# The last six input tiles of the last FFN down-projection as Strassen blocks

## Chip, cores and metric

One Trainium2 chip, one core. The metric is device time of one launch in microseconds (us), the median of several runs.

## What is computed

A two-layer diffusion backbone over 1024 latent tokens and 256 context tokens, model width 1024, everything in float32. Layer 0 mixes tokens with a bidirectional gated linear recurrence, layer 1 with a gated short convolution; each is followed by a gated convolutional FFN (width 2816), and the stream ends in a root-mean-square norm. The part that matters here is the end:

```python
def conv_ffn(h, w_up, conv_w, conv_b, w_down, conv_fn):
    g, v = jnp.split(h @ w_up, 2, axis=-1)
    return (jax.nn.silu(conv_fn(g, conv_w, conv_b)) * v) @ w_down
...
x = x + (gf * conv_ffn(hl, f_w_up[l], f_conv_w[l], f_conv_b[l], f_w_down[l], latent_hconv))
...
return rms_norm(x, final_g)
```

## The kernel before

Activations lie as channels by tokens: `x` is 128 partitions by 8 channel tiles by 1024 tokens, and `H[0]`, `H[1]` are the two halves of 512 tokens. Every matrix product keeps float32 accuracy by splitting both operands into a high and a low part (`split`: ScalarE writes the high part, VectorE the difference), so that `mm` issues three matmuls of 128 x 128 weights with up to 512 tokens each: high-high, high-low, low-high.

Large products go as one level of Strassen's scheme in Winograd's form: `block_items` makes seven weight blocks out of two weight tiles (raw DMA, up to two VectorE additions, then the split), `STEPS` runs the seven products in the order 1, 5, 6, 3, 7, 2, 4, and products 1, 6, 7, 4 add up in one PSUM bank whose running sum is read after each of them. The activation side has seven combinations of four tiles each, named "11", "21", "22", "T1" to "T4"; a table `ROLES` says which product takes which.

The down-projection of the FFN has 22 input tiles. In `v_post`, a pair of gated tiles of the up-projection is turned into its seven combinations by four VectorE subtractions and stored to the DRAM scratch `bd` (`store_blocks`); this is done for the first 16 tiles. The last six are stored plainly to the scratch `ad`. `down` then runs two groups of eight tiles as Strassen blocks (`down_blocks`, four pairs of output tiles each), loading the combinations back through `act_item` (which splits them into operand slots), and finishes with the six left-over tiles by plain products: eight output tiles, each six weight tiles against 512 tokens. In the last layer this rest runs in three pieces, tokens 0 to 511, 512 to 767 and 768 to 1023; the weights of an output tile (768 columns) are loaded and split anew for each piece. After each product, `residual` adds the gated result to `x` on VectorE (a SCALAR_TENSOR_TENSOR from PSUM, called the residual below) and `norm_sq` squares it on ScalarE and adds it on VectorE into `acct`. `final` of a finished piece (sums by matmuls with ones, square root, reciprocal, a broadcast by matmul, four multiplies, four stores) is called while the next piece runs.

No engine runs in program order: the class `Plan` records every operation with an assumed cost, works out for each when it is due (TensorE's order is fixed, and dues run back from it), and emits each engine's instructions in the order that a greedy list schedule gives. The emitted order is then fixed for VectorE, ScalarE, TensorE and the DMA queue of SyncE alike, and each of them works strictly in that order. Line 165 is the place where `Plan` emits, so every profile row carries it; the rows are told apart by tile names: `banks` is PSUM, `wh`/`wl` the split weights, `bh`/`bl` the split activations, `raw` and `s` staging tiles, `xd` the saved stream.

Of the kernel before, what the change touches and what calls it, by code (L numbers as in the profile page):

```python
# [183 lines left out]
def hybrid_kernel(ctx: ExitStack, tc: tile.TileContext, out, xs, cs, c, cc, ada, vecs,  # L184
# [115 lines left out]
    def wsrc(key):  # L300
        kind = key[0]
        if kind in ("x", "xc"):
            return wx[key[1]]
        if kind == "g":
            return wg[key[1]]
        if kind == "o":
            return wo[key[1]]
        if kind == "ri":
            return wri[key[1]]
        if kind == "bo":  # L310
            return wbo[key[1]]
        return wdn[key[1], key[2], :, 2 * D:]

    def dot(dst, raw, bt, eng=None):
# [10 lines left out]
    def weight_item(key):  # L325
        src = wsrc(key)
        n = src.shape[-1]

        def prep(sl, raws):
            hi, lo = flat(sl[0][0], sl[0][2], len(sl))[:, :n], flat(sl[0][1], sl[0][2], len(sl))[:, :n]  # L330
            split(hi, lo, raws[0].tile[:, :n], weight_hi[0])
            return hi, lo
        return Item(key, [Raw(src)], -(-n // HALF), prep)

    def block_items(name, src1, src2, again):

# [114 lines left out]

    accs = {}

    def norm_sq(s, m):
        n = s.stop - s.start
        if m == 0:
            accs[s.start] = acct[:, s.start // HALF, s.start % HALF:s.start % HALF + n]
            act(accs[s.start], x[:, m, s], AF.Square)
        else:
            q = tmp(n)  # L460
            act(q, x[:, m, s], AF.Square)
            if s.start >= 768 and m == KD - 1:
                accs["end"] = q
            else:
                add(accs[s.start], q, accs[s.start], V)
# [621 lines left out]
    def residual(l, sl, m, s, ps, keep):  # L1087
        stt(x[:, m, s], ps, gcol(l, sl, m), x[:, m, s])
        if keep:
            nc.sync.dma_start(xd[:, m, s], x[:, m, s])  # L1090
        norm_sq(s, m)

    def load_res(m):
        nc.sync.dma_start(x[:, m], xd[:, m])
# [60 lines left out]
    def ffn(l, second, i):  # L1155
        cw = [[vcol("f_conv_w", (l * 3 + t) * KFF + j) for t in range(3)] for j in range(KFF)]
        us = []

        def g_post(j0):
            def post(row, h, a, b):  # L1160
                j = j0 + row
                if a is not None:
                    add(a, a, b)
                    b = a
                o = x[:, j % 8, H[h]]
                act(o, b, AF.Identity, bias=vcol("f_conv_b", l * KFF + j), scale=cw[j][1])
# [24 lines left out]

        def store_blocks(q, a, b):

            def put(i, t):
                nc.sync.dma_start(bd[:, i:i + 2, q], t.rearrange("p (h n) -> p h n", h=2))
            b11, b12, b21, b22 = a[:, H[0]], a[:, H[1]], b[:, H[0]], b[:, H[1]]
            nc.sync.dma_start(bd[:, 0, q], b11)
            put(1, b)
            sub(b11, b12, b11)
            sub(b12, b22, b12)  # L1200
            sub(b22, b22, b11)
            sub(b21, b21, b22)
            put(3, a)
            put(5, b)
        for j in range(0, KFF, 2):
            us.append(blocks(("up", l, j), wup[l, j], wup[l, j + 1], g_post(j), 1 if j == 0 else 2 if j == 2 else 0))
            us.append(blocks(("up", l, KFF + j), wup[l, KFF + j], wup[l, KFF + j + 1],
                             v_post(j), 1 if j == 0 else 2 if j == 2 else 0))
        ends = run_blocks(us, second, 8 if l else 24, 2)
        call(gate_bias, l, 5)  # L1210
        return down(l, ends, i)

    def act_item(key, src, load_after, slots, after, pool="raw"):

        def prep(sl, rs):
            for j in (0, 1):
                split(*bslot(slots[j]), rs[0].tile[:, j * HALF:(j + 1) * HALF])
        items[key] = Item(key, [Raw(src, load_after, pool)], 0, prep, after)

    def down(l, ends, i):  # L1220
# [5 lines left out]
        for g in range(2):  # L1226
# [8 lines left out]
            for q in range(4):  # L1235
                steps = down_blocks(l, g, q, role)
                ends = [unit(f, *(acts[p] if q == 0 else []), k) for p, f, k in steps]
        R = released()
# [5 lines left out]
        last, second = i is None, None  # L1244
        if not last:
            begin, first, second = block_norm(i, R[12:] + R[:12])
        pieces = [H[0], slice(HALF, 768), slice(768, SEQ)] if last else H
        for z, s in enumerate(pieces):
            h, o = s.start // HALF, s.start % HALF
            for m in range(KD):  # L1250
                def f(w, m=m, h=h, o=o, s=s):
                    n = s.stop - s.start
                    ps = bank()[:, :n]
                    for k in range(6):
                        rh, rl = bslot(R[6 * h + k])
                        mm(ps, w, slice(k * P, (k + 1) * P), rh[:, o:o + n], rl[:, o:o + n], k == 0, k == 5)
                    residual(l, 5, m, s, ps, not last)
                acts = [("act", l, "t", h, kk) for kk in range(3)] if m == 0 and o == 0 else []
                unit(f, *acts, ("dt", l, m, z))
                if z and last and m == 1:  # L1260
                    fin = final(pieces[z - 1])
                    call(fin[0])
                elif z and last and m == 3:
                    call(fin[1])
                elif z and not last:
                    if m == 0:
                        call(begin)
                    if m == 1:
                        call(norm_cols, i, 1, 0, 1, "norm_mix_g")
                        call(first)  # L1270
        if last:
            for f in final(pieces[-1]):
                call(f)
        return second

    def down_blocks(l, g, q, role):

# [167 lines left out]
```

## Time and profile before

| | us |
|---|---|
| median of 3 runs (lowest to highest) | 2079.51 (2079.14 to 2079.75) |
| profiled execution | 2082.59 |
| its span, first to last instruction | 2080.8 |
| TensorE busy with matmuls in the span | 2036.8 (98%) |
| VectorE busy | 1764.5 (85%) |
| ScalarE busy | 1049.3 (50%) |

The profiled execution is 3.08 us (0.15%) above the median. In the timeline a row has its start, the time it was busy, engine, operation, tiles and shape, how many were merged, and in brackets the idle time before it with what ended it. Instructions of one engine overlap a little, so what one costs its engine is the distance from start to start.

### The profile page before, as it was taken

Reading aid. Unit: us, or ns where it says so; the run is one execution under the profiler, and the core shown is the slowest. Engines: PE = TensorE matmul, PEld = TensorE weight load, DVE = VectorE, ACT = ScalarE, POOL = GpSimd, SP = SyncE. Lnnn points to the kernel's source line nnn. Section 1 sums busy time; section 2 is a strip of 40 time slices with the busy share of each in tenths; the row PEclk is TensorE's granted clock in tenths of the full one; section 3 lists DMA queues with packets and bytes.
Section 4 is the critical chain, followed back from the end, with each engine's and each line's share of the span. In section 5 each row is a group of like instructions: output and inputs, shape, how many; then the busy total and the mean of one; then the engine's idle time right before and its main releaser. Section 6 shows DMA issues by size and latency. Waiting matters only on the chain.

```text
span 2080.8 us, 25029 instructions
## 1 busy us (share of the span) xinstructions
PE 2036.8 (98%) x9218; PEld 1681.5 (81%) x9218; DVE 1764.5 (85%) x2624; ACT 1049.3 (50%) x1574; POOL 0.2 (0%) x4
## 2 busy tenths in 40 slices
PE   8899989999999999999999999999999999999998
PEld 6688877787888888878888788888888888878888
DVE  7998999979888888798769988858988887688867
ACT  6366878546544444535255433435644444464345
POOL 0000000000000000000000000000000000000000
PEclk9999999999999999999999999999999999999999
DMA  7544222551334455565361345652243443474345
GB/s 298 185 169 162 71 81 84 193 167 48 126 132 157 156 174 173 174 199 162 95 194 66 114 164 197 231 192 75 83 136 128 142 137 108 137 236 142 111 140 164
DMA packets 103418, 307.05 MB, mean 148 GB/s; under 512 B 10368, under 2 KB 14720, under 8 KB 103168
## 3 DMA queue, kind: packets, MB, share of 16 engines
q1 hardware_dynamic: 103296, 305.46, 44.6%
q8 instruction: 72, 1.18, 0.2%
q14 instruction: 50, 0.41, 0.1%
HBM read 248.80 MB, written 56.62 MB: 147 GB/s over the span
## 4 chain that ended last, share of the span: by engine, by line
PE 84%; DVE 9%; ACT 4%; DMA 2%; issue 1%; SPq 0%; DVEq 0%; ACTq 0%
PE banks L165 84%; ACT mx L165 2%; DVE x L165 2%; DVE mx L165 2%; DVE u L165 2%; DVE bl L165 2%; DMA x<-in_xs 1%; DVE wl L165 1%; DMA s<-bd 1%; ACT L165 1%; ACT bh L165 1%; DMA raw<-in_wg 0%; DVE uc L165 0%; DVE ul L165 0%; DVE acct L165 0%
## 5 line engine op out<-in xcount | busy, mean ns | idle before, releaser
L165 PE MATMUL banks<-bl,wh 128*128 128x512 f32 (+1 forms) x2720 | 1052.2, 387 | 11.0 <-DVE bl L165 10.9
L165 PE MATMUL banks<-bh,wh 128*128 128x512 f32 (+1 forms) x2720 | 1054.3, 388 | 3.2 <-ACT wh L165 1.6
L165 PE MATMUL banks<-bh,wl 128*128 128x512 f32 (+1 forms) x2720 | 1051.0, 386 | 2.6 <-DVE wl L165 2.5
L165 PEld LDWEIGHTS banks<-bl,wh 128*128 128x128 f32 x2720 | 511.6, 188 | 124.7 <-DVE bl L165 21.6
L165 PEld LDWEIGHTS banks<-bh,wh 128*128 128x128 f32 x2720 | 511.8, 188 | 109.0 <-ACT wh L165 2.0
L165 PEld LDWEIGHTS banks<-bh,wl 128*128 128x128 f32 x2720 | 511.6, 188 | 108.1 <-DVE wl L165 7.3
L165 ACT ACTIVATE wh<-raw 128x512 fp32r<-128x512 f32 (+2 forms) x386 | 275.6, 717 | 475.0 <-PE banks L165 394.7
L165 DVE TENSOR_TENSOR wl<-raw,wh 128x512 fp32r<-128x512 f32 (+2 forms) x386 | 303.2, 794 | 60.4 <-ACT wh L165 56.9
L165 DVE SCALAR_TENSOR_TENSOR x<-banks,mod,x 128x512 f32<-128x512 f32 (+1 forms) x184 | 132.6, 726 | 93.3 <-PE banks L165 92.3
L165 ACT ACTIVATE s<-banks 128x512 f32<-128x512 f32 x174 | 103.8, 596 | 195.0 <-PE banks L165 191.8
L165 ACT ACTIVATE wh<-s 128x512 fp32r<-128x512 f32 x216 | 135.5, 628 | 110.4 <-DVE s L165 63.7
L165 DVE TENSOR_TENSOR wl<-s,wh 128x512 fp32r<-128x512 f32 x216 | 148.5, 688 | 38.6 <-ACT wh L165 34.9
L165 DVE TENSOR_TENSOR s<-s,banks 128x512 f32<-128x512 f32 x158 | 107.8, 683 | 37.4 <-PE banks L165 36.9
L165 DVE SCALAR_TENSOR_TENSOR x<-s,vec,x 128x504 f32<-128x504 f32 x132 | 96.4, 740 | 10.2 <-ACT x L165 9.0
L165 DVE SCALAR_TENSOR_TENSOR acct<-acct,cb 128x1024 f32<-128x1024 f32 x69 | 84.1, 1218 | 4.5 <-DMA acct<-in_ada 4.5
L165 PE MATMUL banks<-uh,wh 128*128 128x512 f32 (+1 forms) x192 | 70.8, 369 | 8.1 <-ACT mx L165 7.0
L165 PE MATMUL banks<-ul,wh 128*128 128x512 f32 (+1 forms) x192 | 70.5, 367 | 3.1 <-DVE ul L165 3.1
L165 PE MATMUL banks<-uh,wl 128*128 128x512 f32 (+1 forms) x192 | 70.2, 366 | 0.0
L165 ACT ACTIVATE bh<-s 128x512 fp32r<-128x512 f32 x88 | 51.5, 624 | 35.3 <-DMA s<-bd 34.0
L165 ACT ACTIVATE bh<-x,cols 128x512 fp32r<-128x512 f32 x64 | 45.1, 721 | 42.1 <-DVE cols L165 27.3
L165 DVE TENSOR_TENSOR x<-x,s 128x512 f32<-128x512 f32 x90 | 61.0, 686 | 0.8
L165 DVE TENSOR_TENSOR bl<-s,bh 128x512 fp32r<-128x512 f32 x88 | 57.2, 684 | 5.0 <-ACT bh L165 5.0
(154 smaller groups left out, 1702.0 us busy)
## 6 DMA issues: line engine op xcount, KB each, us to landing
raw<-in_wup SPq DMA_DIRECT2D x92, 512.0 KB, 3.6
acct<-in_ada SPq DMA_DIRECT2D x69, 512.0 KB, 3.5
bd<-x SPq DMA_DIRECT2D x48, 512.0 KB, 3.2
s<-bd SPq DMA_DIRECT2D x44, 512.0 KB, 4.5
raw<-in_wdn SPq DMA_DIRECT2D x32, 512.0 KB, 4.4
raw<-in_wdn SPq DMA_DIRECT2D x40, 384.0 KB, 3.4
raw<-in_wbi SPq DMA_DIRECT2D x26, 512.0 KB, 4.1
u<-in_ada SPq DMA_DIRECT2D x24, 512.0 KB, 4.6
```

The costliest lines, as they stand in the source:

```text
L165: getattr(getattr(self.tc.nc, e), op)(*a, **k)
```

## The change

Three things belong together. In the last layer `v_post` calls `store_blocks` for the pairs 16, 18, 20 too (`bd` has eleven columns instead of eight). `down` ends for that layer in `last_group`, which runs the six tiles as a Strassen group of three tiles per block: products 1, 2, 6, 7, 4 of the four pairs of output tiles over 512 columns each in an order written out by hand, then products 5 and 3 for tokens 512 to 767 and once more for 768 to 1023. `late_items` prepares 28 weight blocks of 384 columns, with the raw weights of a pair loaded twice, once for products 1, 6, 2, 7, 4 and once for 5 and 3; the eight blocks of 5 and 3 stay in the eight weight slots through both halves. The rows of the weight array are permuted on input. The other layer's code is only moved (`down_rest`).

```diff
-    bd = dp.tile([P, 7, KD, HALF], F32, tag="bd", name="bd")
+    bd = dp.tile([P, 7, KFF // 2, HALF], F32, tag="bd", name="bd")
...
+    def late_items(name, src1, src2):
+        w = src1.shape[-1] // 2
+        raws = [[Raw(src1), Raw(src2)] for _ in range(2)]
...
+                if p in (5, 6):
+                    src = s[0] = stmp("w", w)
+                    add(src, a21, a22)
+                    if p == 6:
+                        sub(src, src, a11)
+                elif p == 7:
+                    src = a21
+                    sub(src, a11, a21)
+                elif p == 3:
+                    src = s[0]
+                    sub(src, src, a11)
+                    sub(src, a12, src)
+                else:
+                    src = {1: a11, 2: a12, 4: a22}[p]
+                split(hi, lo, src)
...
-                if j0 < 16:
+                if j0 < 16 or l:
                     if done[0] + done[1] == 4:
                         store_blocks(j0 // 2, x[:, j0 % 8], x[:, j0 % 8 + 1])
...
+    def last_group(l, ends, stored, last_up):
...
+                ps = st[q, 5 if p in (3, 5) else 1][:, H[p == 2]][:, :n]
+                for k in range(3):
+                    rh, rl = bslot(role3[p][k])
+                    mm(ps, w, slice(k * P, (k + 1) * P), rh[:, o:o + n], rl[:, o:o + n],
+                       p in (1, 2, 5) and k == 0, p in (2, 3, 4) and k == 2, skip_group_check=True)
+                r, h = to[p]
+                t = s if p in (5, 3) else H[h]
+                stt(x[:, 2 * q + r, t], ps, gcol(l, 5, 2 * q + r), x[:, 2 * q + r, t])
+                if p in (2, 4, 5, 3):
+                    end(2 * q + r, t)
...
+        for pq in "10 20 60 11 70 21 40 61 12 71 13 41 62 63 72 73 22 23 42 43".split():
+            put(int(pq[0]), int(pq[1]), H[0])
+        pieces = [slice(HALF, 768), slice(768, SEQ)]
+        for z, s in enumerate(pieces):
+            for n, (p, q) in enumerate(((5, 0), (5, 1), (3, 0), (3, 1), (5, 2), (5, 3), (3, 2), (3, 3))):
+                put(p, q, s)
+                if n == 2:
+                    fin = final(pieces[z - 1] if z else H[0])
                     call(fin[0])
...
+        for f in final(pieces[-1]):
+            call(f)
...
+    last = order[:16] + [16, 18, 20, 17, 19, 21]
```

The instruction order shows two places. The first is VectorE near the end, where the half-width residuals (256 tokens) begin. Before:

```order
L165 SCALAR_TENSOR_TENSOR x<-banks,mod,x 128x256
L165 TENSOR_TENSOR wl<-raw_2695,wh 128x768
L165 RECIPROCAL rt<-rt 128x4
L165 TENSOR_TENSOR s<-eye,rt 128x512
L165 SCALAR_TENSOR_TENSOR x<-banks,mod,x 128x256
L165 TENSOR_TENSOR wl<-raw,wh 128x768
L165 SCALAR_TENSOR_TENSOR x<-banks,mod,x 128x256
L165 TENSOR_TENSOR acct<-s,acct 128x256
L165 TENSOR_TENSOR x<-x,banks 128x2x512 x2
```

And with the change, at the same point:

```order
L165 TENSOR_TENSOR s<-raw 128x384
L165 SCALAR_TENSOR_TENSOR x<-banks,mod,x 128x256
L165 TENSOR_TENSOR wl_2694<-s,wh_2693 128x384
L165 TENSOR_TENSOR wl<-s,wh 128x384
L165 TENSOR_TENSOR s<-s,raw 128x384
L165 TENSOR_TENSOR s<-raw,s 128x384
L165 RECIPROCAL rt<-rt 128x4
L165 TENSOR_TENSOR s<-eye,rt 128x512
L165 TENSOR_TENSOR s<-raw 128x384
L165 SCALAR_TENSOR_TENSOR x<-banks,mod,x 128x256 x2
L165 TENSOR_TENSOR x<-x,banks 128x2x512 x2
L165 TENSOR_TENSOR wl<-s,wh 128x384
```

More and smaller instructions on the weights (`s` and `wl`, 384 columns) now stand between two residuals. The second place is SyncE's DMA queue where the up-projection of the last layer ends and the down-projection begins (`in_wdn` is the down weight). Before:

```order
L165 DMA raw<-bd 128x1024
L165 DMA s<-bd 128x1024
L165 DMA raw_2695<-bd 128x1024
L165 DMA raw<-in_wdn 128x1024
L165 DMA raw<-bd 128x1024
L165 DMA raw_2695<-bd 128x1024
L165 DMA s<-bd 128x1024 x3
L165 DMA raw<-in_wdn 128x1024
L165 DMA ad<-x 128x1024
L165 DMA s<-bd 128x1024
```

And with the change:

```order
L165 DMA raw_2695<-bd 128x1024
L165 DMA raw<-in_wdn 128x1024
L165 DMA raw<-bd 128x1024
L165 DMA raw_2695<-bd 128x1024
L165 DMA bd<-x 128x512
L165 DMA bd<-x 128x2x512
L165 DMA s<-bd 128x1024 x2
L165 DMA bd<-x 128x2x512
L165 DMA s<-bd 128x1024 x3
L165 DMA raw<-in_wdn 128x1024
```

Stores of the last pair's combinations (`bd<-x`) now stand ahead of the loads `s<-bd`, which bring the second half of the first group's activation blocks; one such load stood still earlier before.

## Rows read from the trace of the kernel before

**Rows 1.** The page, part 1: engines, busy time, share of the span.
```profile
PE 2036.8 (98%) x9218; PEld 1681.5 (81%) x9218; DVE 1764.5 (85%) x2624; ACT 1049.3 (50%) x1574; POOL 0.2 (0%) x4
```
**Rows 2.** Chain of waits, last 51 us: start, us, what.
```profile
2029.99 41.20 PE banks L165 x322
```
**Rows 3.** Windows: PE, PEld, DVE, ACT, POOL busy (count), PEclk, DMA share, GB/s.
```profile
1800.00:1850.00 50.00, 50.00 (x222) 41.40 (x222) 35.06 (x54) 26.28 (x45) 0.00 (x0) 1.00 0.53 164
1850.00:1900.00 50.00, 49.71 (x216) 39.52 (x215) 47.01 (x73) 19.82 (x33) 0.00 (x0) 1.00 0.61 205
...
2037.00:2071.20 34.20, 34.20 (x282) 33.66 (x280) 29.21 (x51) 22.36 (x43) 0.00 (x0) 1.00 0.57 181
```
**Rows 4.** Timeline: residuals at full and half width, first half-width matmul.
```profile
2005.55 0.75 DVE L165 SCALAR_TENSOR_TENSOR x<-banks,mod,x 128x512 f32<-128x512 f32 x1 [2.46 <-PE banks L165]
...
2009.63 0.75 DVE L165 SCALAR_TENSOR_TENSOR x<-banks,mod,x 128x512 f32<-128x512 f32 x1 [2.46 <-PE banks L165]
...
2033.90 0.28 PE L165 MATMUL banks<-bh,wh 128*128 128x256 f32 x1
...
2069.05 0.48 DVE L165 SCALAR_TENSOR_TENSOR x<-banks,mod,x 128x256 f32<-128x256 f32 x1 [0.37 <-PE banks L165]
...
2071.21 0.48 DVE L165 SCALAR_TENSOR_TENSOR x<-banks,mod,x 128x256 f32<-128x256 f32 x1 [0.76 <-PE banks L165]
```
**Rows 5.** Timeline of VectorE: neighbours that follow each other without idle time.
```profile
1109.60 2.49 DVE L165 TENSOR_TENSOR wl<-raw,wh 128x512 fp32r<-128x512 f32 x4
1112.01 0.68 DVE L165 TENSOR_TENSOR s<-s,banks 128x512 f32<-128x512 f32 x1
...
1962.32 0.74 DVE L165 SCALAR_TENSOR_TENSOR x<-banks,mod,x 128x512 f32<-128x512 f32 x1
1962.98 0.68 DVE L165 TENSOR_TENSOR raw<-raw,raw 128x512 f32<-128x512 f32 x1
...
2044.47 2.35 DVE L165 TENSOR_TENSOR x<-x,banks 128x1024 f32<-128x1024 f32 x2
2046.73 1.82 DVE L165 TENSOR_TENSOR wl<-raw,wh 128x768 fp32r<-128x768 f32 x2
...
2051.26 0.41 DVE L165 TENSOR_TENSOR acct<-s,acct 128x256 f32<-128x256 f32 x1
2051.59 0.47 DVE L165 SCALAR_TENSOR_TENSOR x<-banks,mod,x 128x256 f32<-128x256 f32 x1
2051.99 0.41 DVE L165 TENSOR_TENSOR acct<-s,acct 128x256 f32<-128x256 f32 x1
```
**Rows 6.** Timeline of VectorE: waits of its own in the last stretch.
```profile
2040.75 0.18 DVE L165 RECIPROCAL rt<-rt 128x4 f32<-128x4 f32 x1 [0.62 <-ACT rt L165]
...
2068.26 0.43 DVE L165 TENSOR_TENSOR acct<-s,acct 128x256 f32<-128x256 f32 x1 [0.15 <-ACT s L165]
```
**Rows 7.** Windows of 2 us around idle times of TensorE in layer 0.
```profile
106.00:108.00 2.00, 1.46 (x7) 0.88 (x5) 1.96 (x3) 1.22 (x2) 0.00 (x0) 1.00 0.97 406
108.00:110.00 2.00, 0.09 (x1) 0.12 (x1) 2.00 (x4) 1.47 (x4) 0.00 (x0) 0.87 0.68 236
...
114.00:116.00 2.00, 2.00 (x6) 1.54 (x5) 1.90 (x5) 1.96 (x4) 0.00 (x0) 0.50 0.15 14
116.00:118.00 2.00, 2.00 (x9) 1.64 (x8) 2.00 (x5) 2.00 (x3) 0.00 (x0) 0.92 0.77 264
366.00:368.00 2.00, 0.87 (x4) 0.65 (x4) 2.00 (x4) 2.00 (x5) 0.00 (x0) 1.00 0.38 110
```
**Rows 8.** Timeline of the DMA queue at the last layer's change from up to down.
```profile
1843.62 3.67 SPq L165 DMA_DIRECT2D s<-bd  x3
...
1849.16 0.42 SPq L165 DMA_DIRECT2D ad<-x  x1
```
**Rows 9.** Waits between 1840 and 1900 us: total, times, longest.
```profile
ACT bh L165 <- DMA s<-bd: 3.6, 3, 2.0
...
PE banks L165 <- DVE bl L165: 0.3, 1, 0.3
```

More of the change, by code (lines that the diff above doesn't have):

```diff
@@ L311, in wsrc @@
             return wbo[key[1]]
+        assert kind == "dt"
         return wdn[key[1], key[2], :, 2 * D:]
@@ L452, in hybrid_kernel, with norm_sq @@
     accs = {}
-    def norm_sq(s, m):
+    def norm_sq(s, m, first, end=False):
         n = s.stop - s.start
-        if m == 0:
+        if first:
             accs[s.start] = acct[:, s.start // HALF, s.start % HALF:s.start % HALF + n]
@@ L461, in norm_sq @@
             act(q, x[:, m, s], AF.Square)
-            if s.start >= 768 and m == KD - 1:
+            if end:
                 accs["end"] = q
@@ L1215, in prep @@
         def prep(sl, rs):
-            for j in (0, 1):
-                split(*bslot(slots[j]), rs[0].tile[:, j * HALF:(j + 1) * HALF])
+            for j, i in enumerate(slots):
+                split(*bslot(i), rs[0].tile[:, j * HALF:(j + 1) * HALF])
         items[key] = Item(key, [Raw(src, load_after, pool)], 0, prep, after)
@@ L1237, in down, with down_rest @@
                 ends = [unit(f, *(acts[p] if q == 0 else []), k) for p, f, k in steps]
+        if i is not None:
+            return down_rest(l, ends, i)
+        last_group(l, ends, stored, last_up)
+    def down_rest(l, ends, i):
         R = released()
@@ L1243, in down @@
                          ends[(sl + 1) // 4])
[L1244 to L1248, printed above, removed]
+        begin, first, second = block_norm(i, R[12:] + R[:12])
+        for z, s in enumerate(H):
             h, o = s.start // HALF, s.start % HALF
@@ L1256, in f @@
                         mm(ps, w, slice(k * P, (k + 1) * P), rh[:, o:o + n], rl[:, o:o + n], k == 0, k == 5)
-                    residual(l, 5, m, s, ps, not last)
+                    residual(l, 5, m, s, ps, True)
                 acts = [("act", l, "t", h, kk) for kk in range(3)] if m == 0 and o == 0 else []
                 unit(f, *acts, ("dt", l, m, z))
-                if z and last and m == 1:
-                    fin = final(pieces[z - 1])
+                if z and m == 0:
+                    call(begin)
@@ new lines, in down_rest, with end, step, f @@
+                if z and m == 1:
+                    call(norm_cols, i, 1, 0, 1, "norm_mix_g")
+                    call(first)
+        return second
+    def last_group(l, ends, stored, last_up):
+        role = roles[0]
+        rel = [(j, ends[t]) for t, (_, n) in enumerate(ROLES) for j in role[n]]
+        role3, acts, need = {}, {}, dict(ROLES)
+        for t, p in enumerate((1, 2, 6, 7, 4, 5, 3)):
+            at = rel[3 * t:3 * t + 3]
+            role3[p] = [j for j, _ in at]
+            acts[p] = [("act", l, 2, p, e) for e in range(2)]
+            for e, sl in enumerate((at[:2], at[2:])):
+                src = bd[:, stored[need[p]], 8:10] if e == 0 else bd[:, stored[need[p]], 10]
+                act_item(acts[p][e], src, last_up if t < 2 else ends[0] - 8, [j for j, _ in sl], sl[-1][1],
+                         "s" if t < 2 else "raw")
+        seen = []
+        def end(m, s):
+            seen.append(s.start)
+            n = seen.count(s.start)
+            norm_sq(s, m, n == 1, s.stop == SEQ and n == KD)
+        for q in range(4):
+            late_items(("db", l, 2, q), *[wdn[l, 2 * q + r, :, 2 * D:] for r in range(2)])
+        st = {}
+        to = {1: (0, 0), 5: (1, 1), 6: (0, 1), 3: (0, 1), 7: (1, 1), 2: (0, 0), 4: (1, 0)}
+        def step(p, q, s):
+            def f(w):
+                n, o = s.stop - s.start, s.start % HALF
+                if p in (1, 5):
+                    st[q, p] = bank()
+                ps = st[q, 5 if p in (3, 5) else 1][:, H[p == 2]][:, :n]
[8 more added lines that the diff above has]
+                    end(2 * q + r, t)
+            return f
+        def put(p, q, s):
+            unit(step(p, q, s), *acts.pop(p, []), ("db", l, 2, q, p))
+        for pq in "10 20 60 11 70 21 40 61 12 71 13 41 62 63 72 73 22 23 42 43".split():
[6 more added lines that the diff above has]
+                    fin = final(pieces[z - 1] if z else H[0])
@@ L1262, in down @@
                     call(fin[0])
-                elif z and last and m == 3:
+                elif n == 4:
                     call(fin[1])
[L1265 to L1274, printed above, removed]
+        for f in final(pieces[-1]):
+            call(f)
```

16 lines of the change are left out of this document (14 added, 2 removed).

## The prediction, made before the changed kernel was run

> **What bounds the kernel.** I read the page first: TensorE's matmuls fill 98% of the span, VectorE 85% [rows 1]. Over the whole kernel TensorE is the bound, and time saved on it should show. The chain of waits agrees: TensorE alone holds the last stretch for 41.20 us without a break, up to 2071.19 [rows 2]. The reader should then look at the stretches that the change touches, because a share over 2 ms hides them. In the windows [rows 3] VectorE is at 47.01 of 50 us where up- turns into down-projection, and at 29.21 of 34.20 over the half-width pieces at the end. TensorE is full in both, but VectorE has only 3 us to spare in the first and 5 us in the second. The change takes work from TensorE and gives work to VectorE in just these two places, so the question is which of them ends last there.
>
> **TensorE's share.** An output tile of 18 full-width matmuls takes 4.08 us, the distance of two residuals that TensorE ends [rows 4]; nine take 2.04. At half width 18 take 2.16 us [rows 4], nine 1.08. Before: 8 x 4.08 + 16 x 2.16 = 67.2 us. After: 20 x 2.04 + 16 x 1.08 = 58.1 us. **Saved: 9.1 us.**
>
> **VectorE's share.** Costs are distances from start to start [rows 5]: 0.60 us for 512 columns (2.41 for four), 0.66 for a residual of 512, 1.13 for 1024, 0.33 and 0.40 for an addition and a residual of 256. An instruction of 384 columns is not in the trace; it lies between 0.33 and 0.60, and I take the middle, 0.47. Added by the change: twelve subtractions in `store_blocks` (7.2 us, in the up-projection), nine more splits of activations (21 slots for 12; 5.4 us), twelve more residuals of 512 (7.9 us). The weights cost about the same in sum (28 splits and 24 additions of 384), but in more pieces, and those of products 5 and 3 come late: their eight slots must be free first.
>
> What matters is when it is due. In the new order of VectorE I counted from the residual of product 7 of the last pair, after which four full and sixteen half units remain on TensorE, up to the last residual. There stand 72 instructions: 6 residuals of 512 (4.0), 15 of 256 (6.0), 11 of 512 columns (6.6), 13 of 256 (4.3), 19 of 384 (8.9), 4 of 1024 (4.5), 2 of 2 x 256, priced as 512 (1.2), and 2 reciprocals (0.4, at 0.2 each by their 0.18 [rows 6]). The sum is 35.9 us. TensorE needs 4 x 2.04 + 16 x 1.08 = 25.4 us, and 2.7 us for the norms' matmuls: today from the first half-width matmul at 2033.90 to 2071.19 it takes 37.3 us [rows 2, 4], of which 16 x 2.16 = 34.6 are products. That makes 28.1 us. So the bound changes: VectorE's queue is 7.8 us longer than TensorE's. Before this point it keeps up: some 25 us of its rows against 15 units of 2.04 us.
>
> VectorE's waits come on top. In the last stretch it waited 0.62 us for ScalarE's square root and 0.15 us for a square [rows 6]; there are two square roots, and the weights of 5 and 3 pass from VectorE to ScalarE and back. Bounds: nothing (all filled by other rows) and 5 us (the idle time of this stretch before, 34.20 - 29.21 [rows 3]). I take 2.5 us, in the middle. **Lost at the end: 10.3 us.** What is late there is `wl` behind the multiplies of `final`, then residuals, for which TensorE waits before it may reuse a bank.
>
> Here a rule speaks for the change and against my sum. The Trainium skill, Perfetto Trace Analysis, "Identifying the Most-Contended Engine", says to relieve the engine of highest occupancy first; by it the 9.1 us would be a gain in full, since TensorE is at 34.20 of 34.20 and VectorE at 29.21. No run so far shows which is right after the change.
>
> **The change from up to down.** The queue of SyncE is strict. In the new order two stores `bd<-x` of the last pair stand before the loads `s<-bd`, and a third between them. The first three loads went out from 1843.62; the first plain store of that pair could go out only at 1849.16 [rows 8], since its data were made then. So the loads, and those behind them, may go out 5.5 us later. They were not early: ScalarE already waited 3.6 us for them, and TensorE lost 0.3 us to the split that follows [rows 9]. VectorE, which also has the last four subtractions (2.4 us) to do, has 3 us of room [rows 3] and cannot make it up. The other eight subtractions fall before 1850, where it was busy 35.06 of 50 us [rows 3], and cost nothing. Bounds: nothing (the queue catches up) and 7 us (5.5 in full, and 1.5 for the subtractions). **Lost: 3.5 us**, the middle.
>
> **TensorE's clock.** After an idle time of some 2.4 us around 108 us the granted clock fell to 0.50 and stayed there until about 116 [rows 7]: half the 2.4 GHz. After 1.1 us (366 to 368) it stayed at 1.00 [rows 7]. At the end one wait could be that long: after the broadcast of the first norm VectorE has two residuals, two multiplies of 1024 and a split to do (0.8 + 2.26 + 0.47 = 3.5 us) before TensorE gets its next weights. Some 6 us at half clock cost 3 us if nothing else waits, and nothing if VectorE is the bound anyway. I take **0.7 us**, nearer to nothing. The Trainium skill, TensorE: Matmul & The Clock Gate, "What's actually happening", also has just two levels and puts the fall down to lack of recent activity; the trace agrees.
>
> After the last residual nothing is changed. In both layers' up-projections the planner moves some stores and subtractions by a few places, because dues shift with the shorter end. I price this at nothing, with 1 us either way: the moved rows feed stores that are read much later, and the spare time of VectorE covers them, as between 1800 and 1850 [rows 3]. If that cover failed, each microsecond late would be one in the total.
>
> **Sum.** -9.1 + 10.3 + 3.5 + 0.7 = +5.4 us. The profiled execution (2082.59 us) is 3.08 us above the median, 2079.51; on the profile's scale this gives 2088.0, on the scale of the runs **2085.0 us**. A measurement of this kernel tells about 0.2% (4.2 us) from no change.
>
> **Rivals.**
> (a) TensorE stays the bound, VectorE's work slips into gaps: 2079.5 - 9.1 = 2070.4, faster. The place is the last 30 us; it decides if VectorE's 72 instructions take under 28.1 us, which would need the price of each to be a fifth lower. For it: VectorE had slack before. This is where the page's rule above would end. Against: 35.9 us by its own rows. Chance 0.06.
> (b) The two stalls eat the gain and no more: with no waits in the last stretch (7.8), none at the turn to down and no slow clock, -9.1 + 7.8 = -1.3, up to +4 when one of the two comes in part: 2078 to 2083.6, no change. For it: the bounds above. Chance 0.24.
> (c) The clock falls in both places and the waits reach their upper ends: -9.1 + 12.8 + 7 + 3 = +13.7, 2093, slower. Against: while TensorE is slow VectorE catches up. Chance 0.05.
> (d) The change doesn't do what it says, for instance if half-width matmuls were held by loading 128 x 128 weights each time. They were of half width before as well, at 0.12 us each, and their number halves; no chance of its own.
> My forecast, VectorE as the bound at the end and a lost microsecond or few at the turn, keeps 0.65: 2083.7 to 2090. Slower by over 0.2%: 0.65 + 0.05 = 0.70; within: 0.24; faster: 0.06. The range from 2079.0 to 2090.5 leaves out (a), (c) and a little of (b).
>
> **What would show it.** Right: at the end VectorE is busy nearly without a break over some 40 us, and TensorE's waits there name `wl`, `x` and `acct` on VectorE, some 10 us in sum; TensorE's busy time falls by about 9 us less what the clock takes; around 1865 TensorE waits a few us for `wh`, `bl` or `x`, behind `s<-bd`. Wrong: TensorE without idle time after 2030, or an end bounded by DMA (late `raw<-in_wdn`), or idle times before 1800 that were not there.

## The result, and the profile after

| | before | changed |
|---|---|---|
| median of the runs | 2079.63 us | 2090.85 us (2086.93 to 2093.60) |
| ratio | 1 | 1.0051, 95% interval 1.0038 to 1.0064 |
| profiled execution, its span | 2082.59, 2080.8 us | 2093.60, 2091.8 us |
| mean granted clock | 0.993 | 0.989 |

By the ratio the change makes the kernel 10.6 us slower (the two medians as they stand differ by 11.2 us), about twice the +5.4 us of the forecast, and the median lies 0.4 us above the upper end of the range. The direction and both places were right; each place cost more.

The page, part 1, of the changed kernel, against [rows 1]:
```profile
PE 2035.9 (97%) x9110; PEld 1675.1 (80%) x9110; DVE 1789.8 (86%) x2685; ACT 1050.7 (50%) x1587; POOL 0.2 (0%) x4
```
TensorE has 108 matmuls less, and yet its busy time falls by 0.9 us where 9 were forecast, less what the clock takes: matmuls that run at half clock count for longer. VectorE has 61 instructions and 25 us more.

To place the loss, three instructions serve as marks that all kernels here have in common: the last reciprocal of 128x4 ahead of the second layer's up-projection, the last residual of 512 before the down-projection's last group (it shows 1.37 us of idle time ahead of it), and the last residual of all. From the timeline of VectorE before (the third mark is in [rows 4]):
```profile
1430.41 0.18 DVE L165 RECIPROCAL rt<-rt 128x4 f32<-128x4 f32 x1 [0.34 <-ACT rt L165]
...
1976.99 0.75 DVE L165 SCALAR_TENSOR_TENSOR x<-banks,mod,x 128x512 f32<-128x512 f32 x1 [1.37 <-PE banks L165]
```
and after, with two residuals of the new units between:
```profile
1427.19 0.18 DVE L165 RECIPROCAL rt<-rt 128x4 f32<-128x4 f32 x1 [0.33 <-ACT rt L165]
...
1978.58 0.75 DVE L165 SCALAR_TENSOR_TENSOR x<-banks,mod,x 128x512 f32<-128x512 f32 x1 [1.37 <-PE banks L165]
...
2007.14 0.75 DVE L165 SCALAR_TENSOR_TENSOR x<-banks,mod,x 128x512 f32<-128x512 f32 x1 [0.63 <-PE banks L165]
2009.17 0.75 DVE L165 SCALAR_TENSOR_TENSOR x<-banks,mod,x 128x512 f32<-128x512 f32 x1 [0.69 <-PE banks L165]
...
2081.49 0.48 DVE L165 SCALAR_TENSOR_TENSOR x<-banks,mod,x 128x256 f32<-128x256 f32 x1
```
A unit of nine takes 2.03 us; 2.04 was priced. Up to the first mark the two profiles differ by 3.2 us in the other direction. From the first to the second mark ("the turn") the time went from 546.58 to 551.39 us, +4.8; from the second to the third ("the end") from 94.22 to 102.91, +8.7; behind the last residual from 9.6 to 10.3.

**The turn.** A window after, against [rows 3] (columns as there), and two short ones:
```profile
1850.00:1900.00 50.00, 47.62 (x195) 36.53 (x194) 43.75 (x69) 21.09 (x36) 0.00 (x0) 0.97 0.66 227
...
1858.00:1860.00 2.00, 2.00 (x6) 1.56 (x7) 1.39 (x3) 1.07 (x2) 0.00 (x0) 0.58 1.02 383
1860.00:1862.00 2.00, 2.00 (x6) 1.41 (x6) 2.00 (x4) 1.01 (x3) 0.00 (x0) 0.57 0.80 256
```
TensorE idles 2.1 us more than before in the first of these, and right behind the longest of its waits (first row below) the granted clock is at 0.58 and 0.57 for four microseconds, which is 1.7 us of clock. Some 1 us of the 4.8 I haven't placed. TensorE's waits, 1840 to 1900, then from 2020 on:
```profile
PE banks L165 <- ACT wh L165: 1.7, 1, 1.7
...
PE banks L165 <- DVE wl L165: 4.3, 2, 2.5
PE banks L165 <- DVE x L165: 2.4, 2, 1.8
PE banks L165 <- DVE acct L165: 2.1, 3, 1.0
PE banks L165 <- DVE s L165: 1.0, 1, 1.0
PE banks L165 <- DVE bl L165: 0.5, 1, 0.5
```
**The end.** These five sum to 10.3 us, all on VectorE, 8.8 of them for the buffers that the prediction named (`wl`, `x`, `acct`). The wait of 1.0 us for `s` stands in the kernel before as well. The chain of waits, which held one piece of TensorE of 41.20 us before [rows 2], changes hands:
```profile
2033.59 5.87 DMA raw<-in_wdn
...
2048.55 0.46 DVE wl L165
...
2050.09 0.60 DVE bl L165
...
2051.16 0.61 DVE acct L165
...
2051.81 7.63 PE banks L165 x28
...
2062.35 6.02 PE banks L165 x34
```
A load of raw weights holds the chain up to 2039, which the prediction had listed as a sign against it (more on it below). From there to 2051 the chain is VectorE almost without a break. Then come 28 matmuls in 7.63 us, and these ran at half clock, as windows of the same stretch show (PEclk is the third number from the end):
```profile
2044.00:2050.00 6.00, 3.52 (x24) 2.96 (x22) 6.00 (x12) 4.86 (x9) 0.00 (x0) 0.95 0.23 66
2050.00:2060.00 10.00, 9.04 (x33) 7.22 (x32) 7.33 (x16) 5.59 (x11) 0.00 (x0) 0.52 0.24 80
2060.00:2066.00 6.00, 3.65 (x18) 3.41 (x19) 5.90 (x12) 1.77 (x4) 0.00 (x0) 0.76 0.47 175
2066.00:2080.00 14.00, 11.48 (x79) 10.88 (x78) 10.35 (x22) 7.23 (x17) 0.00 (x0) 0.87 0.31 112
```
While TensorE crawls, VectorE, the supposed bound, stands and waits for it:
```profile
2057.77 0.48 DVE L165 SCALAR_TENSOR_TENSOR x<-banks,mod,x 128x256 f32<-128x256 f32 x1 [1.34 <-PE banks L165]
2059.47 2.35 DVE L165 TENSOR_TENSOR x<-x,banks 128x1024 f32<-128x1024 f32 x2 [1.22 <-PE banks L165]
```
So the two engines lose time in turn: VectorE makes TensorE wait, the clock falls behind the waits, and the slow matmuls make VectorE wait. Over the 42.0 us from 2039.49 to the last residual VectorE was busy for 35.3, so the sign "nearly without a break" held up to 2056 and not behind it.

### The profile page after: what moved, and what is told of

The parts are those of the page before. It is cut to its first block, busy times and chain, and to the rows that moved or that the text cites. A ratio compares the mean times of both kernels' runs of the same rounds, so it can differ in the third digit from the quotient of the medians.

```text
span 2091.8 us, 24892 instructions
## 1 busy us (share of the span) xinstructions
PE 2035.9 (97%) x9110; PEld 1675.1 (80%) x9110; DVE 1789.8 (86%) x2685; ACT 1050.7 (50%) x1587; POOL 0.2 (0%) x4
## 4 chain that ended last, share of the span: by engine, by line
PE 82%; DVE 10%; ACT 3%; DMA 2%; issue 1%; SPq 0%; DVEq 0%; ACTq 0%
PE banks L165 82%; DVE x L165 2%; DVE bl L165 2%; DVE mx L165 2%; ACT mx L165 2%; DVE u L165 2%; DMA s<-bd 1%; DVE wl L165 1%; DVE acct L165 1%; ACT bh L165 1%; DVE ul L165 1%; ACT L165 0%; DVE s L165 0%; DMA xc<-in_cs 0%; DMA x<-in_xs 0%
## 5 line engine op out<-in xcount | busy, mean ns | idle before, releaser
L165 ACT ACTIVATE wh<-raw 128x512 fp32r<-128x512 f32 (+3 forms) x378 | 263.4, 700 | 449.6 <-PE banks L165 364.9
L165 DVE TENSOR_TENSOR wl<-raw,wh 128x512 fp32r<-128x512 f32 (+3 forms) x378 | 289.1, 774 | 51.8 <-ACT wh L165 47.1
L165 DVE SCALAR_TENSOR_TENSOR x<-banks,mod,x 128x512 f32<-128x512 f32 (+1 forms) x196 | 141.1, 726 | 82.9 <-PE banks L165 82.1
L165 ACT ACTIVATE wh<-s 128x512 fp32r<-128x512 f32 (+1 forms) x228 | 141.8, 622 | 130.8 <-DVE s L165 89.5
L165 DVE TENSOR_TENSOR wl<-s,wh 128x512 fp32r<-128x512 f32 (+1 forms) x228 | 155.1, 681 | 33.5 <-ACT wh L165 29.5
L165 DVE TENSOR_TENSOR x<-x 128x512 f32<-128x512 f32 x100 | 68.4, 686 | 0.8
```

What stands on the lines that cost most here:

```text
L165: getattr(getattr(self.tc.nc, e), op)(*a, **k)
```

## The experiments

The table gives each kernel's median and ratio to before, and from its profile the first mark and the three stretches (us).

| kernel | median, ratio | first mark | turn | end | behind it |
|---|---|---|---|---|---|
| before | 2079.63 | 1430.41 | 546.6 | 94.2 | 9.6 |
| changed | 2090.85, 1.0051 | 1427.19 | 551.4 | 102.9 | 10.3 |
| changed again | 2090.17, 1.0048 | 1430.38 | 551.6 | 97.7 | 10.3 |
| layout | 2085.70, 1.0024 | 1426.83 | 547.5 | 97.7 | 10.3 |
| no multiplies | 2083.07, 1.0013 | 1426.61 | 550.8 | 92.1 | 10.7 |
| additions on GpSimd | 2084.87, 1.0021 | 1429.17 | 551.1 | 93.1 | 10.5 |
| filler, 64 | 2091.39, 1.0052 | 1427.06 | 551.6 | 102.3 | 9.8 |
| filler, 22 | 2089.04, 1.0041 | 1426.80 | 552.2 | 99.2 | 9.9 |
| filler, 38 | 2087.64, 1.0039 | 1430.19 | 552.4 | 97.2 | 10.4 |
| full width | 2088.03, 1.0040 | 1427.06 | 552.4 | 90.2 | 16.5 |
| layout and additions | 2080.61, 1.0002 | 1427.57 | 547.3 | 93.0 | 10.4 |
| halves for one pair | 2079.16, 0.9994 | 1429.80 | 546.8 | 90.0 | 10.5 |
| the same, sum whole | 2077.67, 0.9992 | 1428.14 | 546.8 | 90.2 | 10.4 |
| halves for two pairs | 2077.83, 0.9990 | 1426.21 | 546.8 | 90.2 | 9.8 |

**Layout of the scratch.** Theory: the stores of the last pair stand ahead of loads by a dependency that isn't there. The planner (`Plan.record`) takes an access as the range from its first to its last element; a strided store into `bd` then overlaps the columns of other pairs.
```diff
-    bd = dp.tile([P, 7, KFF // 2, HALF], F32, tag="bd", name="bd")
+    bd = dp.tile([P, KFF // 2, 7, HALF], F32, tag="bd", name="bd")
...
-                nc.sync.dma_start(bd[:, i:i + 2, q], t.rearrange("p (h n) -> p h n", h=2))
+                nc.sync.dma_start(bd[:, q, i:i + 2], t.rearrange("p (h n) -> p h n", h=2))
```
and the loads to match.

> Only the scratch tensor of the up-projection's combinations is laid out anew, with the pair of tiles outermost, so that the stores of the last pair no longer share an address range with the loads of the earlier pairs; nothing of the computation changes. Theory (the turn from up to down is late because SyncE's strict queue holds the stores of the last pair ahead of the loads s<-bd, by a dependency that only the layout makes): the loads go out about 5 us earlier, TensorE's wait for wh around 1865 (1.7 us) goes below 0.5 us, the first residual of the down-projection's last group comes 3 to 5 us sooner than the changed kernel's 1872.49, and the run falls from 2090.9 to 2086 to 2088. Rival (the turn is late because VectorE has twelve more subtractions and the splits of s behind them): the loads go out earlier but TensorE waits as before, the time stays within 1 us of 2090.9.

SyncE's queue in the changed kernel:
```profile
1843.12 2.36 SPq L165 DMA_DIRECT2D bd<-x  x2
1845.53 1.33 SPq L165 DMA_DIRECT2D s<-bd  x2
1847.76 0.37 SPq L165 DMA_DIRECT2D bd<-x  x1
1848.18 6.51 SPq L165 DMA_DIRECT2D s<-bd  x3
```
and with the layout:
```profile
1840.05 3.72 SPq L165 DMA_DIRECT2D s<-bd  x3
...
1845.61 0.42 SPq L165 DMA_DIRECT2D bd<-x  x1
```
The loads went out ahead of the store. Counted from the first mark, they began at 413.2 us, as before the change, against 418.3 in the changed kernel; so they had been 5.1 us late, near the 5.5 that the prediction allowed. TensorE's wait for `wh` was gone (0.5 us in all were left there), and the turn fell from 551.4 to 547.5. The run took 2085.7, 0.3 us under what was expected. A load `s<-bd` took the same time from issue to landing with either layout (median 4.5 us), so it was the order and not the transfers. The order of this queue is nearly all that the turn costs; what is left for the twelve subtractions and nine splits is 0.9 us at most. The clock goes with it: each of the eight profiles with the old layout loses 1.7 us of clock behind the waits at the turn, and none of the five with the new one loses any.

**No multiplies.**
```diff
-                mul(x[:, m:m + w, s], x[:, m:m + w, s], rs.unsqueeze(1).to_broadcast([P, w, n]))
+                if s.start or s.stop != HALF:
+                    mul(x[:, m:m + w, s], x[:, m:m + w, s], rs.unsqueeze(1).to_broadcast([P, w, n]))
```


> Leaves out the four multiplications of the final norm of the first 512 tokens (four instructions of 2 x 512 columns on VectorE, 1.13 us each): that half is stored without the norm's factor. Theory (VectorE's queue is the bound over the last 40 us): 4.5 us less on it are 4.5 us less in the time, and up to 8 us if TensorE then keeps its clock; 2083 to 2086.5, and TensorE's waits after 2020 fall from 10.3 to about 6 us. Rival (TensorE's slower clock or something else than VectorE's amount of work sets the end): less than 1.5 us, 2089.5 to 2091.

2083.07 us, TensorE's waits 6.6 us, as the theory had it. The gain of 7.8 us is more than the 4.5 us taken off VectorE, and the window says why: the clock stayed up over the whole stretch.
```profile
2044.00:2070.00 26.00, 20.67 (x149) 18.48 (x149) 24.61 (x56) 17.48 (x39) 0.00 (x0) 1.00 0.44 150
```
**Additions on GpSimd.** In `late_items` each `add` and `sub` gets the engine `G`:
```diff
-                    add(src, a21, a22)
+                    add(src, a21, a22, G)
```


> The 24 additions and subtractions of 384 columns that build the weights' combinations for the last six tiles run on GpSimd instead of VectorE. Theory (VectorE's queue is the bound at the end): about 11 us (24 x 0.47) leave VectorE, half of them in its last 36 us, so 2083 to 2087, with TensorE's waits after 2020 at about 5 us. Rival (GpSimd takes longer for each, and their splits come late): TensorE waits in the first fifteen units of 2.04 us or in the last sixteen for weights whose releaser is on GpSimd, and the time is 2090 or more.

2084.87, inside the theory's range, though TensorE's waits after 2020 were 6.8 us and not 5. The end took 93.1 us, against 102.9 and 97.7 in the two profiles of the changed kernel. GpSimd took 28.1 us for the 24, over twice VectorE's time for each (the largest of the five groups stands below: busy us, mean ns of one), but no wait of TensorE names it:
```profile
L165 POOL TENSOR_TENSOR s<-raw 128x384 f32<-128x384 f32 x8 | 9.5, 1182 | 2025.6 <-ACT bh L165 1987.3 <-DMA raw<-in_wdn 31.8 <-DVE bl L165 4.3
```
**Filler matmuls**, in three amounts. They write an unused half of a bank; the planner is given no cost for them, so VectorE's and ScalarE's queues stay those of the changed kernel. The largest version puts four into every half-width unit:
```diff
+                if p in (5, 3):
+                    nc.filling = True
+                    for k in range(4):
+                        rh, _ = bslot(role3[p][k % 3])
+                        T.matmul(st[q & 2, 5][:, H[1]][:, :n], w[0][:, :P], rh[:, o:o + n], start=True, stop=True)
```


> Behind the nine products of each half-width unit of products 5 and 3, four further matmuls of 256 columns (some 0.12 us each at full clock) run into an unused half of their bank: 64 in sum, which keep TensorE active where it would wait; the result is not read. Theory (the fall of the granted clock to 0.50 behind several short waits is what made the end cost some 6 us more than the queue of VectorE alone): the clock stays at or near 1.00 from 2050 to 2085 and the time falls by 2 to 6 us, 2085 to 2089. Rival (VectorE alone sets the end, or the clock falls all the same): no gain, from no change up to 7.7 us more (64 x 0.12), 2090 to 2098.

2091.39, in the rival's range; but it can't tell the two apart, because up to 7.7 us of filler stood against whatever the clock gave back, and the clock still fell. Then only where TensorE waited:
```diff
+                if p == 5 and q == 3:
+                    nc.filling = True
+                    for k in range(12 if s.start == HALF else 10):
...
+                extra = {(5, 1, HALF): (0, 12), (3, 0, HALF): (0, 4), (5, 3, HALF): (2, 12), (5, 3, 768): (2, 10)}
```
The first lines are the version with 22, the last that with 38 (product, pair and half; then bank and how many).

> Filler matmuls of 256 columns, not read by anything, at just two places: twelve ahead of product 5 of the last pair in the first half piece, and ten there in the second, about where TensorE waited for wl (2.5 us) and for x (1.8 us) in the changed kernel; at 0.12 us each they take 1.4 and 1.2 us, less than these waits. Theory (the granted clock's fall costs the changed kernel some 4 us: its runs at a mean clock of 0.993 took 2086.9, those at 0.988 and 0.989 took 2090.4 to 2093.6): the clock stays higher from 2058 on, the mean clock is 0.992 or more, and the median falls by 2 to 4 us to 2087 to 2089. Rival (VectorE's queue sets the end at any clock, TensorE's slow matmuls lie beside it): median within 1 us of 2090.9. Second rival (the clock falls before, through the waits around 2045 to 2051, which are not filled): the fall to 0.50 from 2050 on is still there and the median 2090 to 2092.

> The changed kernel again, with the 22 filler matmuls of the earlier run and 16 more: twelve (1.44 us) ahead of product 5 of the second pair in the first half piece, about where TensorE waited 1.8 us for wl at 2045, and four ahead of product 3 of the first pair. Queues of VectorE and ScalarE are unchanged. Theory (the clock costs the changed kernel some 4 us, and falls only through these waits): granted clock 1.00 up to the last residual, mean clock 0.993 or more, median 2086 to 2088, runs within 2 us of each other. Rival (the clock's fall is hidden behind VectorE's queue): 2089 or more, as with 22 fillers.

> The changed kernel itself, unaltered, for a second profile of its end beside more times. The end is measured from the last residual before the stretch that every kernel shares up to the last residual: 102.9 us in the first profile at low clock, 97.2 with fillers in all waits, 94.2 in the kernel before. Theory (the clock falls through the short waits and adds to the end by chance of where it falls): this stretch takes 98 to 103 us, with the granted clock at 0.50 over parts of 2048 to 2066, the turn again 4 to 6 us over the kernel before, and the runs spread over 2087 to 2094. Rival (the fillers helped by something else than the clock, for instance by where banks fall): a profile whose clock stays at 1.00 there and still takes over 101 us.

Windows of the version with 22:
```profile
2044.00:2050.00 6.00, 3.89 (x27) 3.17 (x25) 6.00 (x13) 4.65 (x9) 0.00 (x0) 1.00 0.23 66
2050.00:2058.00 8.00, 6.90 (x29) 6.35 (x30) 6.55 (x14) 4.67 (x9) 0.00 (x0) 0.57 0.31 100
2058.00:2080.00 22.00, 17.96 (x137) 16.56 (x135) 19.56 (x41) 11.56 (x27) 0.00 (x0) 1.00 0.32 119
```
of that with 38:
```profile
2044.00:2054.00 10.00, 9.24 (x60) 8.17 (x59) 10.00 (x19) 6.68 (x12) 0.00 (x0) 1.00 0.34 113
2054.00:2060.00 6.00, 5.44 (x29) 5.05 (x29) 5.55 (x12) 4.72 (x10) 0.00 (x0) 0.72 0.41 134
2060.00:2080.00 20.00, 16.64 (x128) 15.47 (x126) 17.93 (x37) 10.56 (x25) 0.00 (x0) 1.00 0.36 132
```
and of the changed kernel in its second profile:
```profile
2044.00:2054.00 10.00, 7.76 (x46) 6.32 (x44) 10.00 (x20) 6.80 (x12) 0.00 (x0) 1.00 0.32 97
2054.00:2066.00 12.00, 9.32 (x47) 8.53 (x48) 10.67 (x22) 6.76 (x14) 0.00 (x0) 0.72 0.40 149
2066.00:2080.00 14.00, 10.96 (x86) 10.15 (x85) 12.15 (x27) 8.06 (x20) 0.00 (x0) 1.00 0.31 112
```
The sum of (1 - PEclk) x length over such rows is the clock lost: 8.4 us in the first profile of the changed kernel, 3.4 in its second, 3.4 with 22 fillers, 1.7 with 38. The whole ends (102.9, 97.7, 99.2, 97.2) don't follow it closely, because the profiles differ before the clock falls. In the first profile VectorE waited for a load of raw weights, which it did not in the second, and its first residual of 256 came 69.5 us behind the second mark, against 67.9:
```profile
2039.49 0.56 DVE L165 TENSOR_TENSOR s<-raw 128x384 f32<-128x384 f32 x1 [0.97 <-DMA raw<-in_wdn]
...
2048.08 0.47 DVE L165 SCALAR_TENSOR_TENSOR x<-banks,mod,x 128x256 f32<-128x256 f32 x1
```
and in the second
```profile
2049.86 0.48 DVE L165 SCALAR_TENSOR_TENSOR x<-banks,mod,x 128x256 f32<-128x256 f32 x1
```
From this residual to the last one VectorE has the same 56 instructions in the same order in six of the profiles, so this part can be compared (us):

| profile | second mark to first residual of 256 | from there to the last | clock lost |
|---|---|---|---|
| changed | 69.5 | 33.4 | 8.4 |
| changed again | 67.9 | 29.8 | 3.4 |
| layout | 67.6 | 30.1 | 3.4 |
| filler, 22 | 68.8 | 30.4 | 3.4 |
| filler, 38 | 68.2 | 29.0 | 1.7 |
| filler, 64 | 67.7 | 34.5 | 3.4 |

From the first and the fifth row, each microsecond of lost clock costs 0.66 us ((33.4 - 29.0) / (8.4 - 1.7)); the three rows between them would then be 30.1, and stand at 29.8 to 30.4. With none lost this part would take 27.9 us and the whole end 95.5 to 97.4 us, 1.3 to 3.2 over before. This is an estimate; no profile of this queue had its clock at 1.00 throughout. One run supports it: without the four multiplies the clock was never lost and the same part took 23.2 us, 4.7 less than 27.9, for 4.5 us less work. The last row shows why 64 fillers did not help: at the same clock lost they made the part 4.4 us longer than the three rows of 3.4.

The medians are weaker evidence. With 22 fillers the first theory's 2087 to 2089 was just missed (2089.04), and its second rival came true in part: the fall at 2050 stayed, but the median was not 2090 to 2092. With 38 the median was 2087.64 and the clock still fell once, at 2054, so "1.00 up to the last residual" was wrong, as was the spread (one run of five took 2092.0). The changed kernel by itself took 2090.17 in the last series; its second profile came out at 97.7, a little below the 98 to 103 that was expected, with no filler at all. So the falls differ from run to run of one kernel. Its two profiles differ by 5.2 us in the end: 1.6 us stand there before the clock falls, and the other 3.6 come with 5.0 us more of clock lost. What the fillers do is shown for one place only: around 2060 to 2066 both profiles without filler fell and both with 22 and 38 fillers stayed at 1.00, while around 2045 the second profile without filler stayed at 1.00 too. The gain of 38 fillers in the median, 2.5 us, is within the intervals of the ratios (1.0025 to 1.0053 against 1.0034 to 1.0061), so it is not shown.

**Full width for products 5 and 3** undoes the two parts by token halves:
```diff
-        pieces = [slice(HALF, 768), slice(768, SEQ)]
+        pieces = [H[1]]
```


> Undoes the two parts by token halves: products 5 and 3 run once over the second 512 tokens, and the norm of these 512 tokens comes in one piece after the last residual. VectorE loses 8 splits and 12 additions of 384 (20 x 0.47 = 9.4 us) and about 1 us of residuals. The norm behind the last residual works on 512 columns for 256, which I put at 3 to 4 us (10 us to the end before). Theory (VectorE's queue and its weights are what the last 40 us cost): last residual 7 to 9 us sooner, the time 3 to 6 us less than the changed kernel, 2085 to 2088. Rival (the weights made twice are not what holds the end): last residual less than 3 us sooner and the time 2091 to 2094.

2088.03, at the edge of the theory's range. The end fell to 90.2 us, 12.7 less than in the first profile of the changed kernel and 7.5 less than in the second (7 to 9 were expected), and its clock stayed at 1.00 up to 2072; but what stands behind the last residual rose by 6.2 us, not by 3 to 4. VectorE's last rows show it: the broadcast is waited for 2.17 us, and the multiplies take 4.62 us.
```profile
2073.81 0.18 DVE L165 RECIPROCAL rt<-rt 128x4 f32<-128x4 f32 x1 [0.55 <-ACT rt L165]
...
2076.88 4.62 DVE L165 TENSOR_TENSOR x<-x,banks 128x1024 f32<-128x1024 f32 x4 [2.17 <-PE banks L165]
```
So the halves buy 6.2 us behind the last residual and pay for it with weights made twice: 7.0 us (97.2 - 90.2) where 1.7 us of clock are lost, and by the estimate above 5.3 or more (95.5 - 90.2) where none is.

**Layout and additions together**, both edits as above.

> The scratch layout of the second experiment's kind (pair outermost) and the 24 additions on GpSimd together. Theory (two separate places, the turn and the end): the gains add up, -5.2 and -6.0 us from 2090.9, so 2079 to 2081, no change against the kernel before. Rival (both act through the same thing, the clock or the fill of VectorE in the last 40 us, which either alone already frees): 2083 to 2085.

2080.61, in the theory's range: the two gains add up within the noise (-5.2 and -6.0 make 2079.7). They are two places.

**Halves for the last pairs only.** On top of that, products 5 and 3 run at full width but for the last pair or two, and the four multiplies of the first norm stand between units. In the order of units below, `F` is full width, `A` and `B` are the halves, `c` is a call of a norm's part.
```diff
-        pieces = [slice(HALF, 768), slice(768, SEQ)]
+        pieces = [H[1], slice(HALF, 768), slice(768, SEQ), H[0]]
```
```
50F 51F c 30F c 31F c 52F c 32F c 53A 33A 53B c 33B c c c c
50F 51F c 30F c c 31F c 52A c 53A 32A 33A 52B c 53B 32B c 33B c c c
```
The first line of the order is one pair, the second two (the last norm follows both). The first run of one pair left out an addition, and with it the first three pairs' share of the sum of squares of the last 256 tokens.

> Layout and additions as in the experiment that joins them, and two edits more: products 5 and 3 run over token halves for the last pair of output rows alone (full width for the other three pairs: 15 instructions of 384 columns less in splits and additions), and the four multiplies of the first half's norm stand one by one between units, not in a row. Theory (VectorE's queue bounds the end, and single waits under 2 us keep TensorE's clock up): TensorE's waits after 2020 under 7 us, the clock at 1.00 up to the last residual, 2074 to 2078, faster than the kernel before by some 2 to 5 us. Rival (the remaining cost is the latency from the last residual on, and the waits for acct in front of it, which grow as the last pair stands alone): 2079 to 2082.

> As the experiment with halves for one pair, whose sum of squares over the last 256 tokens lacked the first three pairs of rows (one addition of 256 columns on VectorE, 0.33 us, and the act that overwrote it); here the sum is whole. Theory (VectorE's queue at the end, TensorE's clock kept up): 2077 to 2080, within 0.5 us of that run's 2079.2 and 1 to 3 us under the kernel before. Rival (the wait for acct ahead of the last norm is on the path, and the addition lengthens it): 2080 to 2082, no gain against before.

> As the whole version with halves for one pair, but products 5 and 3 run over token halves for the last two pairs of output rows: five more pieces of 384 columns in splits and additions on VectorE and GpSimd, and the norm of the third quarter has four units to hide behind where it had two. Theory (what is left is latency at the end, which more units behind the third quarter's norm hide): 0.5 to 2 us less than one pair. Rival (VectorE's amount of work still counts): 0.5 to 2 us more than one pair.

2079.16, 2077.67 and 2077.83. The first was expected lower, at 2074 to 2078, and came in its rival's range; TensorE's waits (6.0 us) and the clock (1.00 up to the last residual) were as its theory had them. That theory also took single waits under 2 us to be harmless; they were not at the turn of the changed kernel, where the clock fell behind 1.69 us. The second came in its theory's range, though not within 0.5 us of the first. Its stretches are those of the first to 0.2 us, and its ratio is the same within the noise (0.9992 against 0.9994), as the kernel before was 1.2 us faster in its series too (2079.2 against 2080.4). So the whole sum costs nothing that can be seen, and one pair or two are alike: neither theory nor rival of the last came true. Two pairs are the one version measurably under the kernel before (0.9990, interval 0.9981 to 0.9998). Window of its end:
```profile
2040.00:2063.20 23.20, 18.90 (x118) 16.00 (x116) 20.30 (x38) 15.15 (x32) 6.45 (x6) 1.00 0.35 125
```
TensorE still idles 4.3 of 23.2 us, so of the 9.1 us saved on TensorE 4.0 reach the end (94.2 - 90.2), at full clock.

## Why the prediction was right, and where its sizes failed

| term | predicted | measured |
|---|---|---|
| end: TensorE's work and VectorE's queue (-9.1 + 10.3) | +1.2 | +1.3 to +3.2 (estimate at full clock) |
| turn from up to down | +3.5 | +5.1, of which up to 1.7 is clock |
| clock at the end | +0.7 | +1.3 to +3.2 (what the first row leaves of 4.5) |
| behind the last residual | 0 | +0.7 |
| sum | +5.4 | +10.3 |

(The forecast's 2085.0 is 2084.9 by its own numbers, 2079.51 + 5.4.)

*TensorE's share* was right: 2.03 us for a full-width unit. *VectorE's share* was right in its mechanism, and in size as far as the estimate tells: counting its queue from the point where the new work falls due, and adding a wait or two, gave the end at full clock to within 2 us. That the waits were the middle of 0 to 5 us is in part luck. Rival (a), TensorE as the bound, fell with it. The Trainium skill, Perfetto Trace Analysis, "Identifying the Most-Contended Engine", judges TensorE by its weight loads (or its rate of FLOPs) and not by matmul time, which I used: by weight loads it would have relieved TensorE in the last stretch (33.66 against VectorE's 29.21 us), and VectorE at the turn (47.01 against 39.52) and over the kernel (85% against 81%) [rows 1, 3]. In the last stretch the work went to an engine whose queue was then the longer one.

*The turn* was right in its mechanism, the stores ahead of the loads in a strict queue, which the layout shows. Over eight profiles of kernels with the changed kernel's layout of the scratch the stretch takes 551.7 us on average, 5.1 more than before. What I left out is that the clock falls behind the wait itself: 1.7 us of clock are lost in each of the eight. Without them 3.4 us would be left, next to the 3.5 that I took; but I had only taken the middle of 0 to 7 us, so that the size met is luck.

*The clock* is the step that failed. I looked for one wait of some 2.4 us at the end, took 1.1 us to be harmless [rows 7], and gave the term 0.7. In the first profile the clock fell at 2049.5, behind waits of 1.83 and 0.65 us; in the second at 2055.2, behind 0.20, 0.65, 0.81 and 0.57 us in a row, of which the last three are
```profile
2050.48 0.36 PE L165 MATMUL banks<-bh,wh 128*128 128x256 f32 x1 [0.65 <-DVE x L165]
...
2052.53 0.39 PE L165 MATMUL banks<-bl,wh 128*128 128x256 f32 x1 [0.81 <-DVE bl L165]
...
2053.60 1.05 PE L165 MATMUL banks<-ones,acct 128*128 128x1 f32 x8 [0.57 <-DVE acct L165]
```
From the medians, 10.3 us in all (the mean of 1.0051 and 1.0048) less 5.1, 0.7 and 1.3 to 3.2 leave 1.3 to 3.2 us for it at the end, and the two profiles of the changed kernel give 2.2 (0.66 x 3.4) and 5.5 (0.66 x 8.4); with the 1.7 us at the turn it is some 3 to 5 us where I had 0.7. I also reasoned that a slow TensorE costs nothing where VectorE is the bound, and that it would let VectorE catch up; the rows at 2057.77 and 2059.47 show VectorE waiting for the slow matmuls. The Trainium skill, TensorE: Matmul & The Clock Gate, "What's actually happening", puts the fall down to lack of recent activity; the trace agrees, in that each fall stands behind waits and the clock has just two levels (0.50 and 1.00, 1.2 and 2.4 GHz).

*Behind the last residual* I priced nothing, and 0.7 us came (9.8 to 10.7 us over the profiles with halves, against 9.6); the cause stays open.

Rival (b), no change, was excluded by the interval. Rival (c), the clock falling in both places, had the mechanism that happened, and I gave it 0.05; the median lies between my forecast and its 2093, because the waits did not reach their upper ends as well.

## What to carry to other kernels

Work moved from the busiest engine is worth what the next engine can take in that stretch: add up its queue from where the new work falls due. Where waits are expected, price the slow clock with each of them, short ones in a row included, and don't count on the other engine to hide it. A scratch tensor shared by stores and later loads should have the dimension that changes with time outermost, or bookkeeping by ranges makes them wait for each other.

## What was not expected of the hardware

The clock falls behind waits under a microsecond too. With layout and additions, TensorE's row of eight one-column matmuls came after 0.92 us of waiting:
```profile
2044.47 1.05 PE L165 MATMUL banks<-ones,acct 128*128 128x1 f32 x8 [0.92 <-DVE acct L165]
```
and the windows around it went
```profile
2044.00:2046.00 2.00, 1.52 (x13) 1.53 (x14) 2.00 (x5) 1.60 (x5) 0.64 (x1) 1.00 0.16 61
2046.00:2048.00 2.00, 2.00 (x12) 2.00 (x12) 1.75 (x5) 1.99 (x4) 1.92 (x3) 0.53 0.03 8
```
With halves for one pair and the sum whole, the same eight matmuls had no wait ahead of them, and the clock stayed:
```profile
2046.00:2048.00 2.00, 1.49 (x7) 0.90 (x5) 1.07 (x3) 1.97 (x5) 1.25 (x1) 1.00 0.69 190
```
It stayed at 1.00 there although a longer wait followed two microseconds behind them:
```profile
2049.05 1.12 PE L165 MATMUL banks<-s,ones 128*128 128x512 f32 x2 [1.56 <-DVE s L165]
```
So the length of a single wait does not decide by itself; what does is not shown here.

The first mark lies between 1426.21 and 1430.41 us over the profiles, although little ahead of it differs. This spread of 4 us is as large as the effects of single experiments, and it is why the stretches between marks were read beside the medians.
